# A relative-bias table spread through DRAM: one copy from SBUF, or a small write and a copy inside DRAM, issued by another engine

## The chip, the cores and the metric

One core of one Trainium2 chip. The metric is the device time of one execution in microseconds (us); the kernel before was timed in three runs. The engines are PE (TensorE, matmuls), PEld (its weight loads), DVE (VectorE), ACT (ScalarE), POOL (GpSimd) and SP (SyncE). Each engine works through its own queue in order; a DMA is issued by an instruction in the queue of one of them (ACTq is ACT's queue, SPq SP's), and that instruction waits there for whatever the transfer needs.

## What is computed

One decoder layer on 256 tokens of width 2048, all in float32: RMSNorm, one projection, a pooling mixer and a sparse attention side by side, an output projection, a gated feed-forward network with a short convolution, an embedding gate and a last RMSNorm. The change concerns the attention's bias. For every query the 64 best causal keys are selected; the logits of the 8 heads get a T5 bias that depends on the distance alone:

```python
dist = t_pos[None, :, None] - sel
bias = rel_bias[t5_bucket(dist)].astype(jnp.float32)      # rel_bias: (32 buckets, 8 heads)
logits = (jnp.einsum('bqhd,bqkhd->bhqk', qb, k_sel) * (HEAD_DIM ** -0.5)
          + bias.transpose(0, 3, 1, 2))
```

The kernel computes dense logits and masks the keys that are not selected, so it needs the bias of every query p of a block and every key j, in a table T[p, h, j] that holds rel_bias[bucket(p + 128 - j), h].

## The kernel before, in words

The whole layer is a stream of weights. `unit` (lines 59 to 68) loads 512 KB of weights by a DMA from SP into one of four buffers `raw`, and splits them into two parts whose sum is exact: ACT casts `hi` (line 65), DVE subtracts to get `lo` (line 67); both have three buffers. Two units make a column tile of 128 outputs over the 2048 inputs: `cm_matmul` (lines 121 to 127) runs 16 pairs of matmuls, line 125 with hi and line 126 with lo, 8 pairs to a unit. `cm_evict` (line 137) brings a tile out of PSUM through ACT (line 139) and DVE (lines 140, 141). A `raw` buffer is free again when its lo is done, and then SP issues the next load into it.

The order of the stages: first the values and the indexer's keys (lines 202 to 262), then the indexer's query tiles with their scores (`query`, `score`), whose small copies `qs` ACT issues; then 16 tiles of query and key (`qk_tile`), and between them on DVE the eight top-k rounds (`topk_round`, line 339), the mask (`penalty`, which reads `one`, set by GpSimd at line 333) and the logits with their softmax. The pooling mixer and the projections follow. Within each engine the order of instructions is planned at build time by a simulation of the program; the source gives the dependences and the priority.

The bias table stands between the scores and the top-k rounds (lines 320 to 329). One matmul gives `bv`, a row of 384 values for each of 8 heads, on 8 partitions. To get the table, in which each of 128 partitions sees that row shifted by one, the row is written to DRAM 128 times (`bd`, 8 x 128 x 384) and read back with a stride of 383 instead of 384 into `tb`. Both DMAs are issued from ACT's queue. ACT therefore issues the read (line 328) only when the write (line 326) has landed. `tb` is used first in `logits` (line 379), where DVE adds it to the products.

GpSimd does little in this kernel: a few constants, the padding of the pooling stage (lines 441 and 475) and five small powers (line 106).

Of the kernel before, what the change touches and what calls it, by code (L numbers as in the profile page):

```python
# [10 lines left out]
F32 = mybir.dt.float32  # L11
# [7 lines left out]
P = 128  # L19
# [3 lines left out]
NH = 8  # L23
# [5 lines left out]
TOPK = 64  # L29
# [4 lines left out]
NVK = (NH * P + 80) // 3  # L34
UNIT = 3 * NVK

# columns of the packed per-channel parameters
C_GMIX, C_GFFN, C_GPLE, C_PS, C_CONV = 0, 16, 32, 48, 56
# columns of the packed constants
K_ACC0, K_ACC1, K_PEN0, K_PEN1, K_OH, K_INV = 0, 128, 384, 512, 768, 1152  # L40
N_CST = K_INV + 4 * PAD

# [2 lines left out]
def layer(ctx: ExitStack, tc: tile.TileContext, a: dict):  # L45
    nc = tc.nc
    in_order = tc.keep_in_program_order
    V, A, T, G = nc.vector, nc.scalar, nc.tensor, nc.gpsimd
# [8 lines left out]
    aux = ctx.enter_context(tc.tile_pool(name="aux", bufs=4, space=PSUM))  # L57

    def unit(src, n=1024, keep=None):
        """n weight columns on chip as the exact sum hi + lo of two float32r parts"""  # L60
        size, bufs = (1024, 8) if keep else (UNIT, None)
        raw = wraw.tile([P, UNIT], F32, name="raw")
        nc.sync.dma_start(raw[:, :n], src)
        hi = (keep or whi).tile([P, size], F32R, name="hi", bufs=bufs)
        A.copy(hi[:, :n], raw[:, :n])  # L65
        lo = (keep or wlo).tile([P, size], F32R, name="lo", bufs=bufs)
        V.tensor_sub(lo[:, :n], raw[:, :n], hi[:, :n].bitcast(F32))  # L67
        return hi, lo

# [1 line left out]
    prm = cst.tile([P, C_CONV + S], F32, name="prm")  # L71
    nc.sync.dma_start(prm, a["prm"])
    ident = cst.tile([P, P], F32, name="ident")
# [45 lines left out]
        V.tensor_copy(rbc, ps[:, :S])  # L119

    def cm_matmul(ps, hi, lo, kts, first, last):
        """weights stationary: ps[:, :256] + ps[:, 256:] = w.T @ hT"""
        for i, kt in enumerate(kts):
            w = slice(i * P, (i + 1) * P)
            T.matmul(ps, hi[:, w], hT[:, kt, :], start=first and i == 0, stop=False)  # L125
            T.matmul(ps[:, :S], lo[:, w], hT[:, kt, :S],  # L126
                     start=False, stop=last and i == len(kts) - 1)
# [13 lines left out]
        V.tensor_mul(dst, b, rbc)  # L141

    def tm_matmul(pss, hi, lo, act, kts, first, last, toks=(0, 1), n=512, w0=0):
        """activations stationary: pss[t] = act[:, tok t].T @ w"""
        for i, kt in enumerate(kts):
            w = slice(w0 + i * n, w0 + (i + 1) * n)
            for t in toks:
                xh = act[:, kt, t * P:(t + 1) * P]
                xl = act[:, kt, S + t * P:S + (t + 1) * P]
                T.matmul(pss[t][:, :n], xh, hi[:, w], start=first and i == 0, stop=False)  # L150
                T.matmul(pss[t][:, :n], xh, lo[:, w], start=False, stop=False)  # L151
                T.matmul(pss[t][:, :n], xl, hi[:, w], start=False,  # L152
                         stop=last and i == len(kts) - 1)

    def to_hT(n, gcol):
        """columns n*512.. of the residual stream, transposed, times g, split"""
        for kp in range(2):
            ps = aux.tile([P, 512], F32, name="ps")
            for j in range(2):
                kt = 4 * n + 2 * kp + j  # L160
                for t in range(2):
                    T.transpose(ps[:, j * S + t * P:j * S + (t + 1) * P],  # L162
                                x[:, t, kt * P:(kt + 1) * P], ident)
            for j in range(2):
                kt = 4 * n + 2 * kp + j
                split(hT[:, kt, :S], hT[:, kt, S:], ps[:, j * S:(j + 1) * S],
                      prm[:, gcol + kt:gcol + kt + 1])
# [13 lines left out]
    ssq_f = cst.tile([P, 2, 4], F32, name="ssq_f")  # L181
    ssq_p = cst.tile([P, 2, 4], F32, name="ssq_p")

    # =====================================================================
    with ExitStack() as c1:
        ar = c1.enter_context(tc.tile_pool(name="ar", bufs=1))
        catP = ar.tile([P, 8, 2 * S], F32R, name="catP")

# [1 line left out]
        xr = [ar.tile([P, 8, S], F32, name="xr0", tag="tb"),  # L190
              ar.tile([P, 8, S], F32, name="xr1", tag="L1")]
        cc = ar.tile([P, N_CST], F32, name="cc")
# [6 lines left out]
                A.activation(sq, x[:, t, c * 512:(c + 1) * 512], AF.Square,  # L199
                             accum_out=ssq0[:, t, c:c + 1])  # L200

        # the tensor engine's clock rises while the first loads are under way
        warm = aux.tile([P, 512], F32, name="ps")
        pvk = [[(aux if n == 2 else acc).tile([P, 512], F32, name="ps" if n == 2 else "pa")
                for _ in range(2)] for n in range(3)]
# [27 lines left out]
        r_mix = rstd_col(sum4(ssq0), "r_mix")  # L233
        rstd_rows(r_mix)

# [1 line left out]
        kd = ar.tile([P, 2, 2, 64], F32, name="kd")  # L237
        wx = ar.tile([P, 2, IH], F32, name="wx")
        v = ar.tile([P, 2, NH * P], F32, name="v")
# [21 lines left out]
            V.tensor_copy(kx, ps[:, :S])  # L261
            split(kr[:, :S], kr[:, S:], kx)

# [1 line left out]
        s0 = [cc[:, K_ACC0:K_ACC0 + P], cc[:, K_ACC1:K_ACC1 + S]]  # L265
        sc = [ar.tile([P, P], F32, name="sc0"), ar.tile([P, S], F32, name="sc1")]

        def query(ps):
            """fp32 for the first 128 tokens; for the others the rows of a head are followed
            by (or follow) their low parts, so that one product over 128 rows takes both"""  # L270
            qx = ar.tile([P, S], F32, name="qx", bufs=3)
            cm_evict(qx, ps)
            qs = ar.tile([P, P], F32, name="qs", tag="pu", bufs=2)
            nc.scalar.dma_start(qs[64:128], qx[0:64, P:])
            nc.scalar.dma_start(qs[0:64], qx[64:128, P:])
            qh = ar.tile([P, P], F32R, name="qh", tag="pt", bufs=2)
            A.copy(qh, qs)
            qr = ar.tile([P, 2, P], F32R, name="qr", tag="pn", bufs=2)
            for e in range(2):
                own, other = slice(64 * e, 64 * e + 64), slice(64 - 64 * e, 128 - 64 * e)  # L280
                A.copy(qr[own, e, :], qx[own, P:])
                V.tensor_sub(qr[other, e, :], qs[other], qh[other].bitcast(F32))
            return qx, qr
# [32 lines left out]
        for j in range(2):  # L316
            qk_tile(j)
            score(j + 6, qxs[j + 6])

# [1 line left out]
        psb = aux.tile([P, 512], F32, name="ps")  # L321
        T.matmul(psb[:NH, :384], rb, cc[:32, K_OH:K_OH + 384], start=True, stop=True)
        bv = ar.tile([NH, 384], F32, name="bv")
        V.tensor_copy(bv, psb[:NH, :384])
        bd = dram.tile([NH, P, 384], F32, name="bd")
        nc.scalar.dma_start(bd, bv[:, None, :].to_broadcast([NH, P, 384]))
        tb = ar.tile([P, NH, S], F32, name="tb", tag="tb")
        nc.scalar.dma_start(tb, bass.AP(tensor=bd.tensor, offset=bd.offset + 127,
                                        ap=[[383, P], [P * 384, NH], [1, S]]))

# [1 line left out]
        one = ar.tile([P, S], F32, name="one")  # L332
        G.memset(one, 1.0)
        m8, wk, cur = [], [], list(sc)
# [25 lines left out]
            V.scalar_tensor_tensor(pn, gt, BIG, cc[:, k0:k0 + n], op0=OP.mult, op1=OP.add)  # L360
            return pn

# [1 line left out]
        L = [ar.tile([P, NH, P], F32, name="L0"), ar.tile([P, NH, S], F32, name="L1", tag="L1")]  # L364
        nm, sm = [], []
        for t in range(2):
# [63 lines left out]
            po2 = po.rearrange("p (e s) -> p e s", s=S)  # L430
            split(catA[:, h:h + 2, :S], catA[:, h:h + 2, S:], po2)

# [1 line left out]
        plr = None  # L434

        def pooled(g, u):
# [52 lines left out]
            done.append((g, pooled(g, u)))  # L489
        attend(6, pts[6])  # L490

# [1 line left out]
        def out_units(n, pss, gs, first, last):  # L493
            for i, g in enumerate(gs):
                hi, lo = unit(a["w_out"][n][:, g * 1024:(g + 1) * 1024])
# [13 lines left out]
            out_units(n, pss, (4, 5, 6, 7, 0), False, True)  # L509
            out_done(n, pss)  # L510

    # =====================================================================
    pin = ctx.enter_context(tc.tile_pool(name="pin", bufs=1))
    pr = pin.tile([P, 2, S], F32, name="pr")
    nc.scalar.dma_start(pr, a["pT"])
# [2 lines left out]
    with ExitStack() as c2:  # L518
# [23 lines left out]
            V.tensor_mul(ts[0], ts[0], ts[1])  # L542
            split(aT[:, c, :S], aT[:, c, S:], ts[0])

        # the first two tiles leave the last K tiles to the end: those come from the last
        # columns of the residual stream
        ps2 = [acc.tile([P, 512], F32, name="pa") for _ in range(2)]
        for h in range(2):
            for e in range(2):
# [3 lines left out]
        for c in range(1, NF):  # L553
            up_pair(c, [cm_tile(a["w_up"], 2 * c + e) for e in range(2)])

# [1 line left out]
        for n in range(4):  # L557
            pss = [acc.tile([P, 512], F32, name="pa") for _ in range(2)]
            for g in range(NF // 2):
# [2 lines left out]
            add_residual(n, pss, ssq_p)  # L562
            to_hT(n, C_GPLE)

    # =====================================================================
    with ExitStack() as c3:
        gar = c3.enter_context(tc.tile_pool(name="gar", bufs=1))
        pps = {}
# [23 lines left out]
            V.tensor_mul(gx[:, t, c0:c0 + n], xs, gf[:, c0:c0 + n])  # L592

        def store(t, slots):
            """the last slot joins the sum of those before it"""
            ms = gar.tile([P, 1], F32, name=f"ms{t}")
            V.tensor_scalar(ms, ssq_o[:, t, slots - 1:slots], seen[:, t:t + 1], 1.0 / D,
                            op0=OP.add, op1=OP.mult)
            r = rstd_of(ms, f"r_o{t}")
            for h in range(4):  # L600
                sl = gx[:, t, h * 512:(h + 1) * 512]
                if h % 2 == 0:
                    V.tensor_scalar(sl, sl, r, None, op0=OP.mult)
                else:
                    A.activation(sl, sl, AF.Copy, scale=r)
                eng = nc.sync if h % 2 == 0 else nc.scalar
                eng.dma_start(a["out"][t * P:(t + 1) * P, h * 512:(h + 1) * 512], sl)
# [31 lines left out]


def _cm(w):
    """(K, C) -> (C/128, 128, K/128*128): rows of a partition for one column tile together"""
    k, c = w.shape
    return np.ascontiguousarray(
        w.reshape(k // P, P, c // P, P).transpose(2, 1, 0, 3).reshape(c // P, P, k))


def _tm(w, n=512):
    """(K, N) -> (N/512, 128, K/128*512)"""
    k, c = w.shape  # L650
    return np.ascontiguousarray(
        w.reshape(k // P, P, c // n, n).transpose(2, 1, 0, 3).reshape(c // n, P, k // P * n))
# [72 lines left out]
```

## Time and profile before

| what | value |
|---|---|
| timed runs: median (lowest to highest) | 1234.42 us (1234.06 to 1234.61) |
| profiled execution: span from first to last instruction | 1232.6 us |
| busy: PE, DVE, ACT, POOL | 97%, 66%, 51%, 0% |
| moved by DMA | 230.44 MB, 187 GB/s in the mean |
| mean granted TensorE clock | 0.989 |

The profile is of one execution of its own; its span leaves out what lies before the first and after the last instruction, so it is a little shorter than the timed runs. [...] A view of the instructions in time has one row for each: start in us, duration in us, engine, source line, operation, result<-operands, shapes, and in brackets how long the engine had been idle before it and what ended that.

### The profile page before, as it was taken

How to read it: one execution, taken by the hardware profiler on the slowest of the kernel's cores; microseconds unless marked ns; L12 is line 12 of the kernel's file. 1: busy time of each engine (PE TensorE's matmuls, PEld its weight loads, DVE VectorE, ACT ScalarE, POOL GpSimd, SP SyncE). 2: the span in 40 equal slices, each digit the busy share in tenths (PEclk: the TensorE clock that was granted, in tenths of full speed). 3: DMA queues.
4: the chain of work that ended last, by engine and by line, in shares of the span. 5: the costliest groups of instructions: out<-in, count | busy, mean ns of one | idle time of the engine just before them, and what ended most of it. 6: DMA issues, size and time to landing. Idle time of an engine off the chain costs nothing.

```text
span 1232.6 us, 16720 instructions
## 1 busy us (share of the span) xinstructions
PE 1199.4 (97%) x6332; PEld 1027.0 (83%) x6332; DVE 816.1 (66%) x1234; ACT 625.5 (51%) x951; POOL 5.5 (0%) x23
## 2 busy tenths in 40 slices
PE   9999669999999999999999999999999999999996
PEld 8988558888888888888888888888888888888886
DVE  6566465796555877787777877788645454545565
ACT  7455134565454655555555555555434343434453
POOL 0000000000000000000000000000000000000000
PEclk9999879999999999999999999999999999999998
DMA  9654555545655655555555565566666666666662
GB/s 352 222 185 146 126 171 191 161 148 178 188 173 168 210 190 189 189 188 189 189 189 190 189 190 190 191 189 192 189 188 185 190 182 191 181 194 213 188 217 87
DMA packets 67784, 230.44 MB, mean 187 GB/s; under 512 B 7416, under 2 KB 11128, under 8 KB 67576
## 3 DMA queue, kind: packets, MB, share of 16 engines
q1 hardware_dynamic: 63488, 223.88, 57.8%
q10 hardware_dynamic: 4216, 5.51, 2.1%
q8 instruction: 49, 0.80, 0.3%
q14 instruction: 31, 0.25, 0.1%
HBM read 225.16 MB, written 3.67 MB: 186 GB/s over the span
## 4 chain that ended last, share of the span: by engine, by line
PE 95%; DMA 3%; ACT 1%; DVE 0%; SPq 0%; issue 0%; POOLq 0%; ACTq 0%
PE pa L125 35%; PE pa L126 18%; PE pa L151 12%; PE pa L152 12%; PE pa L150 12%; DMA bd<-bv 3%; PE ps L151 1%; PE ps L152 1%; PE ps L150 1%; PE ps L162 1%; DMA raw<-in_w_first 0%; PE ps L465 0%; PE ps L290 0%; ACT hi L65 0%; PE ps L375 0%; PE ps L291 0%
## 5 line engine op out<-in xcount | busy, mean ns | idle before, releaser
L67 DVE TENSOR_TENSOR lo<-raw,hi 128x1024 fp32r<-128x1024 f32 (+2 forms) x417 | 508.5, 1220 | 373.5 <-ACT hi L65 370.6
L65 ACT CAST hi<-raw 128x1024 fp32r<-128x1024 f32 (+2 forms) x417 | 435.8, 1046 | 555.3 <-issue 218.7
L125 PE MATMUL pa<-hT,hi 128*128 128x512 f32 x1904 | 667.8, 394 | 20.3 <-ACT hi L65 20.3
L126 PE MATMUL pa<-hT,lo 128*128 128x256 f32 x1904 | 534.5, 281 | 0.5 <-DVE lo L67 0.5
L125 PEld LDWEIGHTS pa<-hT,hi 128*128 128x128 f32 x1904 | 358.4, 188 | 102.4 <-ACT hi L65 21.0
L126 PEld LDWEIGHTS pa<-hT,lo 128*128 128x128 f32 x1904 | 358.6, 188 | 1.2 <-DVE lo L67 1.0
L152 PE MATMUL pa<-hi,aT 128*128 128x512 f32 x352 | 138.4, 393 | 0.0
L151 PE MATMUL pa<-lo,aT 128*128 128x512 f32 x352 | 138.3, 393 | 0.0
L150 PE MATMUL pa<-hi,aT 128*128 128x512 f32 x352 | 125.9, 395 | 0.0
L151 PEld LDWEIGHTS pa<-lo,aT 128*128 128x128 f32 x352 | 66.0, 188 | 15.6
L152 PEld LDWEIGHTS pa<-hi,aT 128*128 128x128 f32 x352 | 66.0, 188 | 15.1
L150 PEld LDWEIGHTS pa<-hi,aT 128*128 128x128 f32 x352 | 66.1, 188 | 15.0
L151 PE MATMUL pa<-lo,hT 128*128 128x512 f32 (+2 forms) x208 | 74.4, 358 | 0.1
L152 PE MATMUL pa<-hi,hT 128*128 128x512 f32 (+2 forms) x208 | 74.3, 358 | 0.0
L150 PE MATMUL pa<-hi,hT 128*128 128x512 f32 (+2 forms) x208 | 64.4, 359 | 1.4 <-ACT hi L65 1.4
L532 ACT ACTIVATE cv<-ub,cnv 128x256 f32<-128x256 f32 x88 | 52.6, 598 | 1.0 <-DVE ub L141 1.0
L140 DVE TENSOR_TENSOR eb<-pa,eb 128x256 f32<-128x256 f32 x119 | 49.6, 417 | 0.0
L536 DVE SCALAR_TENSOR_TENSOR cv<-ub,cnv,cv 128x256 f32<-128x256 f32 x88 | 42.6, 485 | 3.0
L150 PEld LDWEIGHTS pa<-hi,hT 128*128 128x128 f32 x208 | 38.3, 188 | 7.2 <-ACT hi L65 2.0
L151 PEld LDWEIGHTS pa<-lo,hT 128*128 128x128 f32 x208 | 39.1, 188 | 5.7 <-DVE lo L67 0.7
L139 ACT COPY eb<-pa 128x256 f32<-128x256 f32 x119 | 43.5, 365 | 0.0
L152 PEld LDWEIGHTS pa<-hi,hT 128*128 128x128 f32 x208 | 39.1, 188 | 5.0
(171 smaller groups left out, 822.2 us busy)
## 6 DMA issues: line engine op xcount, KB each, us to landing
raw<-in_w_up SPq DMA_DIRECT2D x176, 512.0 KB, 3.8
raw<-in_w_down SPq DMA_DIRECT2D x88, 512.0 KB, 3.6
raw<-in_w_qk SPq DMA_DIRECT2D x32, 512.0 KB, 3.9
raw<-in_w_out SPq DMA_DIRECT2D x32, 512.0 KB, 3.7
raw<-in_w_pg SPq DMA_DIRECT2D x32, 512.0 KB, 3.9
raw<-in_w_first SPq DMA_DIRECT2D x15, 552.0 KB, 6.4
raw<-in_w_qi SPq DMA_DIRECT2D x16, 512.0 KB, 4.6
raw<-in_w_u SPq DMA_DIRECT2D x16, 512.0 KB, 3.7
```

Of the source, the lines that this page charges most:

```text
L65: A.copy(hi[:, :n], raw[:, :n])
L67: V.tensor_sub(lo[:, :n], raw[:, :n], hi[:, :n].bitcast(F32))
L125: T.matmul(ps, hi[:, w], hT[:, kt, :], start=first and i == 0, stop=False)
L126: T.matmul(ps[:, :S], lo[:, w], hT[:, kt, :S], start=False, stop=last and i == len(kts) - 1)
L139: A.copy(b, ps[:, S:])
L140: V.tensor_add(b, ps[:, :S], b)
L150: T.matmul(pss[t][:, :n], xh, hi[:, w], start=first and i == 0, stop=False)
L151: T.matmul(pss[t][:, :n], xh, lo[:, w], start=False, stop=False)
L152: T.matmul(pss[t][:, :n], xl, hi[:, w], start=False, stop=last and i == len(kts) - 1)
L162: T.transpose(ps[:, j * S + t * P:j * S + (t + 1) * P], x[:, t, kt * P:(kt + 1) * P], ident)
L532: A.activation(t, u[:, 2:], AF.Identity, bias=cnv[:, k + 3:k + 4], scale=cnv[:, k + 2:k + 3])
L536: V.scalar_tensor_tensor(t, u[:, :S], cnv[:, k:k + 1], t, op0=OP.mult, op1=OP.add)
```

## The change

The row of 384 values is written to DRAM once for each head (`bs`, 12 KB). A second DMA copies it 128 times, from DRAM to DRAM, into `bd`; its source repeats through a dimension of step 0, as before. The third reads the table back shifted, as before. All three are issued from GpSimd's queue. The rest of the diff takes away comments and docstrings.

```diff
         bv = ar.tile([NH, 384], F32, name="bv")
         V.tensor_copy(bv, psb[:NH, :384])
+        bs = dram.tile([NH, 384], F32, name="bs")
+        nc.gpsimd.dma_start(bs, bv)
         bd = dram.tile([NH, P, 384], F32, name="bd")
-        nc.scalar.dma_start(bd, bv[:, None, :].to_broadcast([NH, P, 384]))
+        nc.gpsimd.dma_start(bd, bs[:, None, :].to_broadcast([NH, P, 384]))
         tb = ar.tile([P, NH, S], F32, name="tb", tag="tb")
-        nc.scalar.dma_start(tb, bass.AP(tensor=bd.tensor, offset=bd.offset + 127,
+        nc.gpsimd.dma_start(tb, bass.AP(tensor=bd.tensor, offset=bd.offset + 127,
                                         ap=[[383, P], [P * 384, NH], [1, S]]))
```

## Rows read from the trace of the kernel before

**Rows 1.** The page: busy us, share of the span, instructions, by engine.
```profile
PE 1199.4 (97%) x6332; PEld 1027.0 (83%) x6332; DVE 816.1 (66%) x1234; ACT 625.5 (51%) x951; POOL 5.5 (0%) x23
```
**Rows 2.** The page: busy tenths and granted clock in 40 slices.
```profile
PE   9999669999999999999999999999999999999996
...
PEclk9999879999999999999999999999999999999998
```
**Rows 3.** The chain that ended last, its longest pieces: start, us, what.
```profile
126.62 35.03 DMA bd<-bv
```
**Rows 4.** ACT's instructions in time, 126 to 163 us.
```profile
126.62 1.30 ACTq L326 DMA_DIRECT2D bd<-bv  x1
128.94 1.05 ACT L65 CAST hi<-raw 128x1024 fp32r<-128x1024 f32 x1 [3.09 <-PE pa L125]
...
134.51 1.05 ACT L65 CAST hi<-raw 128x1024 fp32r<-128x1024 f32 x1 [1.45 <-issue]
161.67 0.41 ACTq L328 DMA_DIRECT2D tb<-bd  x1
162.20 1.04 ACT L65 CAST hi<-raw 128x1024 fp32r<-128x1024 f32 x1 [26.64 <-DMA bd<-bv]
```
**Rows 5.** DVE's instructions in time: three lo, first use of tb.
```profile
130.02 1.23 DVE L67 TENSOR_TENSOR lo<-raw,hi 128x1024 fp32r<-128x1024 f32 x1 [1.00 <-ACT hi L65]
...
135.91 1.21 DVE L67 TENSOR_TENSOR lo<-raw,hi 128x1024 fp32r<-128x1024 f32 x1
...
163.28 1.23 DVE L67 TENSOR_TENSOR lo<-raw,hi 128x1024 fp32r<-128x1024 f32 x1 [24.65 <-ACT hi L65]
...
222.68 0.69 DVE L379 SCALAR_TENSOR_TENSOR L<-ps,tb 128x512 f32<-128x512 f32 x1 [0.77 <-PE ps L375]
```
**Rows 6.** PE's instructions in time around the gap.
```profile
135.32 0.39 PE L125 MATMUL pa<-hT,hi 128*128 128x512 f32 x1
...
142.70 0.40 PE L125 MATMUL pa<-hT,hi 128*128 128x512 f32 x1
...
163.30 0.79 PE L125 MATMUL pa<-hT,hi 128*128 128x512 f32 x1 [20.08 <-ACT hi L65]
164.56 0.58 PE L126 MATMUL pa<-hT,lo 128*128 128x256 f32 x1 [0.47 <-DVE lo L67]
164.94 0.63 PE L125 MATMUL pa<-hT,hi 128*128 128x512 f32 x1
...
168.55 0.39 PE L125 MATMUL pa<-hT,hi 128*128 128x512 f32 x1
```
**Rows 7.** Stretches: us; busy by engine; granted clock, share of DMA engines, GB/s.
```profile
146.00:150.00 4.00, 0.00 (x0) 0.00 (x0) 0.00 (x0) 0.00 (x0) 0.00 (x0) 0.72 0.50 148
...
155.00:160.00 5.00, 0.00 (x0) 0.00 (x0) 0.00 (x0) 0.00 (x0) 0.00 (x0) 0.50 0.45 49
...
163.00:166.80 3.80, 3.03 (x8) 2.24 (x9) 3.52 (x10) 2.69 (x5) 0.00 (x0) 0.50 1.00 321
172.00:190.00 18.00, 18.00 (x106) 15.79 (x106) 14.00 (x29) 8.15 (x11) 0.00 (x0) 1.00 0.60 195
```
**Rows 8.** The DMA issue of tb, its landing; landings of all 16 copies qs.
```profile
tb<-bd ACTq DMA_DIRECT2D x1, 1024.0 KB, 5.5
...
DMA to landing us min/median/max: 1.8/2.1/4.8
```
**Rows 9.** POOL's instructions in time: `one`, and the first after 126 us.
```profile
1.05 0.31 POOL L333 MEMSET one<- 128x256 f32 x1
...
251.32 0.12 POOL L441 MEMSET pn<- 128x32 f32 x1 [125.87 <-DVE pn L442]
```
**Rows 10.** Weight loads of line 63: landings in 60:126; issue and landing in 131:134.
```profile
DMA to landing us min/median/max: 3.6/3.8/5.1
...
L63 SPq DMA_DIRECT2D raw<-in_w_qk x1: 328/328/328, 131.3 to 131.3; - x1
...
DMA to landing us min/median/max: 18.1/18.1/18.1
```

## The prediction, made before the change was run

> **What bounds the kernel now.** I read the busy shares first [rows 1]: PE is busy 97% of the 1232.6 us span, so time can only be won where PE idles or runs at a low clock. The digits by slice of 30.8 us say where [rows 2]: PE's fifth and sixth slice (123 to 185 us) are sixes among nines, like the tail, and PEclk has its 8 and 7 in the same two. The chain of waits names the cause [rows 3]: one piece of 35.03 us, the transfer bd<-bv, from 126.62 us on.
>
> The instructions of that stretch show how a DMA came to stand on PE's path. ACT issues bd at 126.62, does three more weight casts, from 128.94 to 134.51 and so one every 2.8 us, and then stands idle for 26.64 us [rows 4]: its queue holds the issue of tb<-bd, which may not start before bd has landed, and behind it the next cast, hi of line 65. DVE then has no hi to subtract and waits for ACT too: its next lo runs at 163.28 [rows 5]. [...]
>
> **What the wait costs.** Pairs of matmuls (line 125, then 126) start at 135.32 and at 142.70 with 20 pairs between them, 21 steps, so 7.38 / 21 = 0.351 us a step [rows 6]. The next pair was due at 142.70 + 0.351 = 143.05. It starts at 163.30 but has its lo only at 164.56; the second starts at 164.94, and the eighth at 168.55, six steps later. Without the wait the eighth would start at 143.05 + 7 x 0.351 = 145.51. The stretch loses 168.55 - 145.51 = **23.04 us**. The six steps took 3.61 us and not 2.11, so 1.5 us of that is low clock there, 1.8 with the first pair's share; the rest is waiting.
>
> **The change, part by part.**
>
> *ACT's two issues go.* This is the gain: behind 134.51 the next casts are due at 137.3, 140.1 and 142.9, and no wait on bd stands before them. ACT's own saving, 1.30 + 0.41 us of issuing [rows 4], is worth nothing: ACT idled 3.09 us for PE before the cast at 128.94.
>
> *The small write bs<-bv is added*, 12 KB. The nearest row is qs<-qx, 32 KB, which lands in 2.1 us in the median, 1.8 to 4.8 [rows 8]. I take 3 us, with these ends. It lies beside everything and only delays bd.
>
> *bd now reads DRAM and not 8 partitions of SBUF.* In 155 to 160 us, with the weight loads stalled behind ACT, bd alone keeps 0.45 of the 16 engines (7.2) busy and moves 49 GB/s; in 163 to 166.8, with tb and weights, the share is 1.00 at 321 GB/s [rows 7]. A busy engine moves 6.8 GB/s there and 20 here: bd crawled, and its 8 source rows set it apart. The upper end is that it keeps its 35.0 us; the lower that it goes at tb's rate, 1024 KB in 5.5 us [rows 8], so 1536 KB in 8.3. I take that rate on half of the engines, 16.5 us, since the outer dimension is still 8 and tb is the row with a DRAM source.
>
> *The issues wait on GpSimd.* Queued behind them are the memsets of the pooling stage; the first POOL instruction after 126 us runs at 251.32, and the memset of `one`, which top-k needs, ran at 1.05 [rows 9]. So a POOL that waits for tens of us holds nobody up, and SP's queue is not passed. How long GpSimd takes to issue is shown nowhere; the nearest rows are ACT's 0.41 and 1.30 us. I take 2 us each; the upper end is the second rival's.
>
> *Is tb there in time?* Its first use is the addition of line 379 at 222.68 [rows 5], which moves to 222.68 - 23.04 = 199.6. The chain by my values: 126.6 + 3 + 16.5 + 5.5 + 3 x 2 = 158; with bd at its old 35.0 it is 176. Either leaves over 20 us.
>
> *Do the weight loads still come?* This is what is late next. The load issued at 131.3, beside bd, landed after 18.1 us; 20 loads before took 3.8 in the median [rows 10]. ACT's wait hid that. This load refills the buffer that lo read at 130.02, so it feeds the fourth cast after 128.94, due at 140.1. The lo of 135.91 to 137.12 served the last 8 pairs, from 143.05 - 8 x 0.351 = 140.24: 3.1 us of cushion. The pairs of the cast due at 140.1 start one unit (8 pairs, 2.81 us) after 143.05, at 145.86, and cast and lo take 2.3 us, so the load has to land by 143.5, 12.2 us after its issue. It landed at 149.4, that is 21 us after bd began to move (126.6 + 2), 0.63 of the transfer's 33 us. With bd at 16.5 us from 131 on, the same share gives 131 + 10.4 = 141.4: in time, by 2 us. I cost it at nothing; what it costs if that cover goes is the first rival.
>
> [...]
>
> **The sum.** Against the profiled execution's span: 1232.6 - 23.0 = 1209.6. The median of the timed runs, 1234.42, lies 1.8 above this span, and I let that stand: 1234.42 - 23.04 = **1211.4 us**, 1209 to 1214 by itself.
>
> **Rivals.**
>
> *The copy still crowds out the loads.* If bd still moves for 33 us, the load of 131.3 lands at 149.4 again and its lo ends at 151.7, where PE wanted it at 145.86: 5.9 us of waiting and up to 1.8 of low clock, so 1211.4 + 7.7 = 1219, and 1222 if bs's 3 us come on top. For it: the landing of 18.1 us, and the outer 8 unchanged. Against it: the rate per engine of the reads from DRAM, three times higher.
>
> *tb comes too late: slower than before.* bd and tb are 1024 pieces each (8 x 128 rows of 1536 bytes, 128 x 8 of 1024). If GpSimd builds them slowly, line 379 holds DVE, and every lo behind it, from 199.6 on. With X = landing - 199.6 and the 3.1 us of cushion, PE loses X - 3.1 + 1.8. That equals the 23.0 saved at X = 24.3, a landing at 223.9, 97 us after the start of the chain: some 47 us for each of the two, 46 ns a piece. At 55 us each the landing is at 239.6, the loss 38.7 and the time 1250. For it: no row bounds GpSimd's issuing. Against it: a chain of 31 us by my values where 97 decide, and 1.3 ns a piece in ACT's issue of bd (1.30 us for 1024).
>
> [...]
>
> *It does nothing.* The order is planned anew, and another DMA wait may hold ACT at the same place, or line 379 may move ahead of tb. Then 1232 to 1236. Against it: after the change ACT's queue holds no wait on a DMA in this stretch but for its weights.
>
> **Chances.** Forecast 0.68; loads crowded out 0.20; tb late 0.07, nearly all of it slower; nothing 0.05, of which 0.02 still faster. A measurement here tells about 0.2%, 2.5 us, from no change. Faster 0.90, same 0.03, slower 0.07. The range 1209 to 1222 takes in the forecast and most of the first rival, some 0.85.
>
> **What would show it.** Right: no 35 us piece in the chain; no idle of ACT that ends with bd; PE nines and PEclk 9 in the fifth and sixth slice; line 379 without an idle on tb, near 199.6; POOL's issues near 127, 131 and 150. Wrong by the first rival: raw loads near 130 us that land after more than 12 us, and ACT idle on them. Wrong by the second: DVE idle at line 379 until tb lands, and a PE gap behind 200 us. If the step of the pairs outside the stretch changes, or span and median part by more than 1.8 us, my account of where the time goes is not complete.

## The result, and the profile after

| kernel | median (lowest to highest) | ratio to before, 95% interval |
|---|---|---|
| before | 1234.51 us (1234.06 to 1235.13) | |
| changed | 1211.02 us (1210.77 to 1211.86) | 0.9815 (0.9803 to 0.9826) |

The forecast was 1211.4 us. The span of the profiled execution went from 1232.6 to 1209.0 us. (One of the six executions of the experiment e7 below, the profiled one, ran at a mean granted clock of 0.751 and took 1474.04 us; its time is left out, and only its transfers are read from that trace.)

Busy tenths and granted clock (tenths of full speed) of the changed kernel, in 40 slices, against [rows 2]:

```profile
PE   9999999999999999999999999999999999999996
...
PEclk9999999999999999999999999999999999999998
```

The two sixes of PE and the dip of the clock are gone; the tail's six is as before. ACT's instructions in time, against [rows 4]:

```profile
133.82 1.05 ACT L65 CAST hi<-raw 128x1024 fp32r<-128x1024 f32 x1 [1.46 <-PE pa L125]
136.88 1.05 ACT L65 CAST hi<-raw 128x1024 fp32r<-128x1024 f32 x1 [2.01 <-PE pa L125]
...
139.69 1.05 ACT L65 CAST hi<-raw 128x1024 fp32r<-128x1024 f32 x1 [1.49 <-PE pa L125]
142.49 1.05 ACT L65 CAST hi<-raw 128x1024 fp32r<-128x1024 f32 x1 [1.75 <-PE pa L125]
```

Where ACT stood for 26.64 us there is a cast about every 2.8 us, each released by PE: ACT runs ahead and waits for PE to free a buffer, not for a DMA. The wait itself has moved to POOL, with the three issues:

```profile
126.24 0.71 POOL L326 DMA_DIRECT2D bs<-bv  x1 [1.44 <-DVE sc L299]
129.23 1.11 POOL L328 DMA_DIRECT2D bd<-bs  x1 [2.28 <-DMA bs<-bv]
145.49 0.93 POOL L330 DMA_DIRECT2D tb<-bd  x1 [15.15 <-DMA bd<-bs]
227.62 0.12 POOL L443 MEMSET pn<- 128x32 f32 x1 [81.20 <-DVE pn L444]
```

POOL waits 15.15 us for bd, and its next instruction is due 80 us later. The issues of the page (KB each, us to landing), the landings of the weight loads issued in 126 to 140 us, and the stretch 129 to 145, to set beside [rows 7, 8, 10]:

```profile
bd<-bs POOLq DMA_DIRECT2D x1, 1536.0 KB, 16.0
tb<-bd POOLq DMA_DIRECT2D x1, 1024.0 KB, 6.2
...
bs<-bv POOLq DMA_DIRECT2D x1, 12.0 KB, 2.7
...
DMA to landing us min/median/max: 6.5/7.8/7.8
...
129.00:145.00 16.00, 16.00 (x94) 14.03 (x93) 15.40 (x47) 6.40 (x9) 1.11 (x1) 1.00 0.72 243
```

bd takes 16 us and not 35, tb is there at 145.49 + 6.2 = 151.7 us, loads beside bd land after 7.8 us and not 18.1, and PE is busy for 16.00 of 16.00 us. Its pairs, and the first use of tb (now line 381), answer to [rows 6] and the last of [rows 5]:

```profile
142.41 0.39 PE L125 MATMUL pa<-hT,hi 128*128 128x512 f32 x1
...
144.86 0.40 PE L125 MATMUL pa<-hT,hi 128*128 128x512 f32 x1
...
198.97 0.69 DVE L381 SCALAR_TENSOR_TENSOR L<-ps,tb 128x512 f32<-128x512 f32 x1 [0.77 <-PE ps L377]
```

The pair that started at 168.55 starts at 144.86, 23.69 us earlier. 23.04 of that is the stretch; the other 0.65 us was already won when it began (142.41 stands where the prediction has 143.05). I take that part for chance: the chain's first piece, the loads raw<-in_w_first from 2.6 us on, took 5.90 us before and 5.24 after, and 5.41 and 5.46 us in the traces of e6 and e11 below.

### The profile page after: what moved, and what is told of

Read it like the earlier page. It is cut to its first block, busy times and chain, and to the rows that moved or that the text cites. A ratio compares the mean times of both kernels' runs of the same rounds, so it can differ in the third digit from the quotient of the medians.

```text
span 1209.0 us, 16727 instructions
## 1 busy us (share of the span) xinstructions
PE 1197.5 (99%) x6332; PEld 1027.2 (85%) x6332; DVE 817.0 (68%) x1234; ACT 625.4 (52%) x951; POOL 8.5 (1%) x26
## 4 chain that ended last, share of the span: by engine, by line
PE 98%; ACT 0%; DMA 0%; DVE 0%; SPq 0%; issue 0%; POOLq 0%; ACTq 0%
PE pa L125 36%; PE pa L126 19%; PE pa L152 12%; PE pa L151 12%; PE pa L150 12%; PE ps L151 1%; PE ps L152 1%; PE ps L150 1%; PE ps L162 1%; PE ps L290 1%; PE ps L467 0%; DMA raw<-in_w_first 0%; PE ps L377 0%; PE ps L291 0%; PE ps L125 0%; PE ps L428 0%
```

## The experiments

The changed kernel and all the experiments have the order of instructions on PE and DVE that the kernel before has, so no new plan plays a part (e10 has other shapes around one matmul). ACT's and POOL's orders differ by the DMAs that are named, in e10 also by a memset and a small copy on POOL, in e7 also by one ACT instruction of the last stage. Each ratio is to the kernel before, timed beside the experiment (medians of 1234.16 to 1234.52 us). Theory A is the prediction's; theory B puts the whole gain down to the faster copy.

**e1, the issuer alone**

```diff
-        nc.scalar.dma_start(bd, bv[:, None, :].to_broadcast([NH, P, 384]))
+        nc.gpsimd.dma_start(bd, bv[:, None, :].to_broadcast([NH, P, 384]))
...
-        nc.scalar.dma_start(tb, ...)
+        nc.gpsimd.dma_start(tb, ...)
```

> Only the issuer changes: the copy bd still reads the 8 partitions of SBUF, with no small write before it, but both DMAs are issued by GpSimd. Theory A (the 23 us were ACT's wait for bd in front of its casts): ACT does not wait, so 1211 to 1213 us if the weight loads beside bd land within 12 us, as they did in the changed kernel (7.7 to 7.8 us), and 1219 to 1222 us if they land after 17 to 18 us, as beside the old bd; bd itself takes 33 to 36 us either way, and tb lands near 170, before line 379 wants it near 199. Theory B (the gain is the faster copy, by its DRAM source): bd is as slow as before, so most of the loss stays, 1228 to 1235 us.

Measured: 1226.84 us (1226.37 to 1227.23), ratio 0.9937 (0.9925 to 0.995). A miss for both: between A's 1219 to 1222 and B's 1228 to 1235. ACT's row and the landings of the loads issued in 129 to 140 us say whose mechanism it was:

```profile
153.19 1.04 ACT L65 CAST hi<-raw 128x1024 fp32r<-128x1024 f32 x1 [15.12 <-DMA raw<-in_w_qk]
...
DMA to landing us min/median/max: 22.6/26.3/26.8
```

ACT waits for raw, not for bd. This is A's mechanism, the crowding of the first rival, at a larger price than I gave it: the slow copy delays the loads even more from GpSimd's queue (22.6 to 26.8 us here) than from ACT's (16.2 to 18.3 us in e3 below).

**e2, the source alone** (the changed kernel with `nc.scalar` for all three DMAs)

> Only the source changes: small write, copy inside DRAM and read back, all three issued by ACT. Theory A: ACT waits for bd in front of the cast that is due at 137. With bd landing 16 us after its issue near 129.3, as in the changed kernel, that cast starts near 146.5 instead, its lo ends near 149 where PE wants it near 142.5: some 6 us of waiting and up to 1.8 us of low clock, 1217 to 1220 us. With a copy that lands in 8 to 10 us ACT would still wait, but within the cushion: 1211 to 1213 us. Theory B: the faster copy is the whole gain, 1211 us, whatever ACT does.

Measured: 1216.65 us (1214.77 to 1217.51), ratio 0.9853 (0.984 to 0.9866). ACT, then PE, then the loads:

```profile
143.74 0.40 ACTq L330 DMA_DIRECT2D tb<-bd  x1
144.26 1.04 ACT L65 CAST hi<-raw 128x1024 fp32r<-128x1024 f32 x1 [8.86 <-DMA bd<-bs]
...
145.36 0.49 PE L125 MATMUL pa<-hT,hi 128*128 128x512 f32 x1 [2.30 <-ACT hi L65]
146.62 0.39 PE L126 MATMUL pa<-hT,lo 128*128 128x256 f32 x1 [0.77 <-DVE lo L67]
...
DMA to landing us min/median/max: 6.5/6.7/6.8
```

Theory B falls: the copy is fast (14.6 us), the loads land in time, and 5.6 us of the gain are still missing by the medians, because ACT stands behind the issue of tb. (The profiled execution, 1214.77 us, has the lowest of the four times.) bd landed somewhat earlier than I had assumed, so the time is just under the range given.

**e3, the wait alone** (the kernel before, with only `nc.gpsimd` for tb)

> Only the issue of tb moves to GpSimd; bd is still issued by ACT and still reads SBUF, as before the change. Theory A with the first rival of the prediction: ACT waits no more for bd, but the weight loads issued beside it land after 17 to 18 us where 12.2 are allowed; 5.9 us of waiting and up to 1.8 of low clock are left, 1217 to 1222 us, and ACT idles for raw and not for bd. If the landings of 17 to 18 us only came from ACT's standing still: 1211 to 1213 us. Theory B: the copy is as slow as before, 1228 to 1235 us.

Measured: 1219.16 us (1218.44 to 1222.53), ratio 0.9884 (0.9869 to 0.99). ACT, then PE, then the loads:

```profile
148.82 1.04 ACT L65 CAST hi<-raw 128x1024 fp32r<-128x1024 f32 x1 [10.79 <-DMA raw<-in_w_qk]
...
149.92 0.79 PE L125 MATMUL pa<-hT,hi 128*128 128x512 f32 x1 [4.71 <-ACT hi L65]
...
DMA to landing us min/median/max: 16.2/17.7/18.3
```

This is the first rival, and its total is as priced (1219): without ACT's wait the crowded loads become the bound. Its terms come out less well: PE waits 4.71 us where 5.9 were priced, and the rest of the 7.7 us by which the span exceeds the changed kernel's, priced at 1.8, fits the low clock behind the wait (0.50 in 148 to 153 us). The landings of 17 to 18 us before were real and not an effect of ACT's standing still.

**e5, the table late by three slow copies** (e1, with the copy from SBUF issued three times)

> The table made late: GpSimd issues the copy from SBUF into bd three times, each after the one before has landed, then the read back; the extra copies write the same values again. The planned order of PE, DVE and ACT is that of the changed kernel. By the second rival's price: three copies of 35 to 36 us and 7 us for the read put the landing of tb at 235 to 242, line 379 wants it at 199, so X is 36 to 43 and PE loses X - 3.1 + 1.8: 1246 to 1254 us, slower than before the change, with DVE idle on tb. If a late tb were hidden by other work (other cushions than the 3.1 us): 1211 to 1235 us.

Measured: 1266.95 us (1266.03 to 1269.04), ratio 1.0265 (1.0251 to 1.0279). The time missed the range, and the mechanism was not the one tested. POOL's issue of tb and line 380:

```profile
237.61 0.93 POOL L329 DMA_DIRECT2D tb<-bd  x1 [35.90 <-DMA bd<-bv]
...
254.25 0.69 DVE L380 SCALAR_TENSOR_TENSOR L<-ps,tb 128x512 f32<-128x512 f32 x1 [0.77 <-PE ps L376]
...
DMA to landing us min/median/max: 6.0/26.7/29.4
```

tb landed at 237.61 + 6.6 = 244.2, before it was wanted, since the three copies had crowded out the loads for 110 us (landings of 26.7 us in the median, 165 to 215 us) and held everything back: 56 us over the changed kernel for three copies, where e1 has 15.8 for one. It says nothing on a late table, so e11 was made.

**e6, only the waiting DMA on GpSimd** (the changed kernel, with `nc.scalar` for bs and bd)

> The changed kernel with bs and bd issued by ACT again and only tb, the DMA that waits for bd, issued by GpSimd. Theory A (a wait for bd in front of ACT's casts, and a source so slow that it crowds out the weight loads, are the two things to be rid of; who issues bs and bd does not count): ACT's own wait is the one for bs, over near 129 where no cast is due before 131.5, and loads beside bd land in 6.5 to 6.8 us as with the source alone: 1210.5 to 1212.5 us. Rival (GpSimd's queue for the copy itself matters, for the loads beside it): 1215 to 1219 us, as with the source alone.

Measured: 1210.61 us (1210.36 to 1210.82), ratio 0.9808 (0.9795 to 0.9822). Of the three issues that moved, one counts, that of tb.

**e7, an outer dimension of 128**

```diff
-        bd = dram.tile([NH, P, 384], F32, name="bd")
-        nc.gpsimd.dma_start(bd, bs[:, None, :].to_broadcast([NH, P, 384]))
+        bd = dram.tile([P, NH, 384], F32, name="bd")
+        nc.gpsimd.dma_start(bd, bs[None, :, :].to_broadcast([P, NH, 384]))
```

(The strides of the read tb<-bd change with the layout.)

> The changed kernel with bd laid out as 128 x 8 x 384, so that the copy inside DRAM has an outer dimension of 128 and not 8. If half of the engines carried bd because of the outer 8, it now lands 8 to 11 us after its issue and not 16, and the read back starts near 139. Both theories: bd lies beside other work and line 379 has 40 us to spare, so 1210.5 to 1212.5 us; if the denser copy crowds the weight loads past 12 us, 1212 to 1216 us.

Measured: 1210.67 us (1210.53 to 1211.44), ratio 0.981 (0.9797 to 0.9824). bd landed after 8.2 us and not 16.0. The reading that an outer dimension of 8 leaves part of the engines idle fits: before a load moves beside it, the copy of the changed kernel reaches 209 GB/s at 0.60 of the engines (132 to 133 us), this one 356 GB/s at all of them (155 to 156 us of its trace). That half of them stay idle, as the prediction and the expectation have it, was an estimate. The halving of the time is not all the layout's, since fewer loads moved beside the copy in e7: taking off its 1.57 MB, they had about 45 GB/s (152.5 to 160.5 us), against some 145 GB/s in 129 to 145 us of the changed kernel. The time does not notice.

**e8, three copies inside DRAM** (the changed kernel, with bd<-bs issued three times)

> The changed kernel with the copy inside DRAM issued three times into bd, each after the one before has landed; the planned order of PE, DVE and ACT is unchanged. It triples the copy's time and bytes. Theory A: loads beside it land in 8 us, under the 12 us that they may take; tb lands near 129 + 3 x 16.3 + 7 = 185, 14 us before line 379 wants it: 1210.5 to 1213 us. Rival (the copy still costs something by crowding, hidden in the result because the rest gained more than 23 us): 2 us or more on top for each copy, 1215 us or more.

Measured: 1210.79 us (1210.56 to 1211.31), ratio 0.981 (0.9797 to 0.9824).

```profile
bd<-bs POOLq DMA_DIRECT2D x3, 1536.0 KB, 16.9
```

50 us of copying cost nothing that can be measured. The copy is hidden, with room for two more.

**e9, no GpSimd, the issue later in ACT's queue** (e2, with the issue of tb pinned ahead of `qk_tile(2 + r)` at r = 5)

> No GpSimd at all: small write, copy inside DRAM and read back all issued by ACT, but the issue of tb stands nine casts later in ACT's queue, near 162 us, when bd has landed (143.7 us with the source alone). Theory A: it is the place of the wait in a queue that counts, not the engine: 1210.5 to 1212.5 us. Rival (ACT's queue is the wrong one because of its issuing or of its DMA queue): 1215 to 1219 us, as with the source alone.

Measured: 1210.91 us (1210.52 to 1211.21), ratio 0.9811 (0.9797 to 0.9824). The issue stood some three casts earlier than I had placed it, at 154.5 us:

```profile
154.37 1.05 ACT L65 CAST hi<-raw 128x1024 fp32r<-128x1024 f32 x1 [1.77 <-PE pa L125]
154.50 0.44 ACTq L397 DMA_DIRECT2D tb<-bd  x1
...
157.12 1.05 ACT L65 CAST hi<-raw 128x1024 fp32r<-128x1024 f32 x1 [1.44 <-PE pa L125]
```

bd has landed by then and the casts keep their step. The engine is not what counts; a wait in front of work that is due is.

**e10, the 8 rows on spread partitions** (e1, with the heads on partitions 0, 4, ... 28)

```diff
+        rw = ar.tile([32, NH, 4], F32, name="rw")          # zeros, rb copied to rw[:, :, 0]
...
-        T.matmul(psb[:NH, :384], rb, cc[:32, K_OH:K_OH + 384], start=True, stop=True)
+        T.matmul(psb[:32, :384], rw.rearrange("p h e -> p (h e)"), cc[:32, K_OH:K_OH + 384],
+                 start=True, stop=True)
...
-        nc.gpsimd.dma_start(bd, bv[:, None, :].to_broadcast([NH, P, 384]))
+        nc.gpsimd.dma_start(bd, bv[0:32:4, None, :].to_broadcast([NH, P, 384]))
```

> The copy bd from SBUF again, issued by GpSimd, with no small write: the kernel of the issuer alone (1226.8 us), but the 8 rows of bv lie on partitions 0, 4, 8, ... 28 and not on 0 to 7 (a memset, a small copy and 32 columns instead of 8 in one weight load are added). [...] If any copy from SBUF to DRAM of this shape crawls, or any 8 partitions do: bd lands after 35 us as before and the time is 1225 to 1229 us.

Measured: 1211.03 us (1210.03 to 1211.31), ratio 0.9811 (0.9798 to 0.9825), and not the 1225 to 1229 us of a copy that crawls from any 8 partitions. The copy, the stretch 129 to 133 us, and the loads issued in 129 to 140:

```profile
bd<-bv POOLq DMA_DIRECT2D x1, 1536.0 KB, 12.9
...
129.00:133.00 4.00, 4.00 (x25) 3.55 (x24) 4.00 (x12) 1.32 (x2) 0.00 (x0) 1.00 0.73 270
...
DMA to landing us min/median/max: 4.2/5.8/8.1
```

Against e1 only the partitions differ: 12.9 us for 35.9, and 15.8 us of time. In 130 to 131 us, while no load moves, the copy alone keeps 0.50 of the engines busy at 203 GB/s; the old one, alone, kept 0.45 busy at 49 [rows 7]. The crawl came from 8 neighbouring partitions, not from SBUF as a source, and DRAM as a source is one cure of two.

**e11, the table late without crowding** (the changed kernel, with bd<-bs issued again by ACT at `j == 12` of the last `qk_tile` loop, tb by GpSimd behind it)

> The table made late without crowding out the loads: the changed kernel, with the copy inside DRAM issued a second time, by ACT near 183 us, and tb by GpSimd behind it (the second copy writes the same values). The planned order of PE, DVE and all casts is that of the changed kernel. bd lands near 198, tb near 207; line 379 wants tb at 199 and holds DVE, so X is 7 to 10. By the second rival's price PE loses X - 3.1 and up to 1.8 of low clock: 1215 to 1220 us, with DVE idle on tb's landing. If DVE has more cushion there than 3.1 us: 1211 to 1214 us.

Measured: 1217.80 us (1216.45 to 1218.39), ratio 0.9864 (0.9851 to 0.9878). DVE, then PE:

```profile
197.21 1.23 DVE L67 TENSOR_TENSOR lo<-raw,hi 128x1024 fp32r<-128x1024 f32 x1 [0.81 <-ACT hi L65]
208.09 0.69 DVE L379 SCALAR_TENSOR_TENSOR L<-ps,tb 128x512 f32<-128x512 f32 x1 [9.66 <-DMA tb<-bd]
...
210.70 0.58 PE L126 MATMUL pa<-hT,lo 128*128 128x256 f32 x1 [5.02 <-DVE lo L67]
```

DVE waits for tb 9.66 us where 0.77 are usual: X = 8.9, and the second rival's price is 8.9 - 3.1 + 1.8 = 7.6 us; the kernel lost 6.8 against the changed one. PE itself waited 5.02 us for a lo, so the cushion here was 3.9 us and not the 3.1 of another place that the price takes; some 1.8 us are left for the low clock (0.66 in 205 to 215 us).

## Why the prediction was right

- *The wait behind tb's issue is the loss, 23.04 us.* Shown: the pair of 168.55 starts 23.69 us earlier, 0.65 of it from the start of the run; the medians part by 23.49 us. The low clock, about 1.8 us of it (0.50 in 163 to 166.8 us before [rows 7], 1.00 in 129 to 145 us after), went with the wait. Nothing else moved: from that pair to the end of the span it is 1064.1 us in both profiles (1232.6 - 168.55 and 1209.0 - 144.86), a pair still takes 0.35 us (142.41 to 144.86, seven steps), and the profiled execution's own time, 1210.77 us, is 1.8 above its span.
- *Two things had to go.* The prediction kept them apart: ACT's wait, and the loads beside bd. Without the wait alone 8.1 us stay over the changed kernel (e3), with the fast source alone 5.6 (e2), with both nothing (e6, e9). The gains do not add, 15.4 + 17.9 for 23.5, since the two losses lay over each other.
- *Terms of the sum.* bs 3 us, measured 2.7; bd 16.5, measured 16.0; tb 5.5, measured 6.2; issues 2 each, measured 0.7 to 1.1. tb landed at 151.7 where 158 was forecast and 199 allowed. That bd came out to half a microsecond is in part luck: I took half of tb's rate, some 95 GB/s, while the copy reaches 209 GB/s before a load moves beside it (132 to 133 us) and then shares the engines with the loads, which the estimate did not have. A load was allowed 12.2 us to land, I expected about 10 (131.3 to 141.4), and the longest took 7.8. That estimate erred to the safe side: it scaled the old landing with the copy's length.
- *The first rival was real*, and the part of the change that changes the source is what removed it. Another issuer for the slow copy did not lift the contention (e1: loads of 22.6 to 26.8 us). What I had not foreseen is that it made it worse, 1226.8 against 1219.2 us in e3.
- *Why bd crawled*: I had only "its 8 source rows set it apart". e10 makes it their place: from every fourth partition the copy alone moves 203 GB/s with 0.50 of the engines busy, where from 8 neighbours it moved 49 with 0.45 [rows 7]; over e10's whole 12.9 us, beside loads, it is 122. Why the place counts no run shows.
- *The second rival did not occur, and its price holds* (e11: 6.8 us for 7.6). GpSimd's issue of bd, 1024 rows of 1536 bytes, took 1.11 us, in a stretch (129 to 145 us) in which DVE was busy for 15.40 of 16.00 us.

## What to carry to other kernels

Before a DMA is issued from an engine that feeds the critical path, look for the DMA that it waits for: everything behind it in that queue waits too (26.64 us here), and either another queue or a place further down the same one is enough. A wait can hide a second bound: the idle times of the profile showed only the first, the landing times of the transfers beside it showed the second, and both had to be mended. A small source in SBUF that one DMA reads many times should not lie on neighbouring partitions (shown here for 8 rows: 49 GB/s, and 203 when they are four apart).

## What the runs showed of the hardware that was not expected

- A copy from 8 neighbouring partitions to DRAM, which moves only 49 GB/s, delays other queues' loads: 512 KB loads that land in 3.8 us took 16 to 18 us beside it when ACT issued it (e3), and 23 to 27 us when GpSimd did (e1). Why GpSimd's is worse these runs do not settle. The traces show one difference: in e1 the copy moves in packets of 4608 bytes that take 734 ns in the median, in e3 in packets of 1536 bytes that take 227 ns.
- Rows on every fourth partition instead of neighbouring ones took the same copy from 35.9 to 12.9 us, and in stretches where it moves alone from 49 to 203 GB/s, at 0.45 and 0.50 of the engines.
- A copy inside DRAM of 1536 KB went from 16.0 to 8.2 us with an outer dimension of 128 in place of 8, in part because fewer loads moved beside it; alone, its rate went from 209 GB/s at 0.60 of the engines to 356 at all of them.
